# Seven-product down projection for the last row slice too, and two of the seventh slice's column slices put behind the last up projection

## The chip, the cores and the metric

The kernel runs on one core of a Trainium2 chip. The metric is the device time of one execution in microseconds; lower is better. Times of whole runs are medians of several executions; the profile is of one execution of its own.

## The reference, cut to what matters

A trunk of two pre-norm residual layers over x of 256 tokens by 2048 features in float32: the first mixes tokens with a convolution module, the second with a state-space layer, and each is followed by an MLP with 8192 hidden features. A last RMS norm ends it. Only the MLP of the second layer and the last norm are touched:

```
def mlp(h, w_up, w_down):
    a = jax.nn.relu(h @ w_up)          # 256 x 8192
    return (a * a) @ w_down            # 256 x 2048

x = x + mlp(rms_norm(x, mlp_norm[1]), w_up[1], w_down[1])
return rms_norm(x, final_norm)
```

## The kernel before, in words

**Products.** All weights stream from HBM in float32. Each tile is split into a high part (`hi`, a rounded copy made by ScalarE, L143) and a low part (`lo`, the difference, made by VectorE, L150). Every product is then three matmuls: high by high, high by low, low by high. The steps of the program are a list; one step is one tile of 1 MiB (128 partitions by 2048 numbers), fetched and split in two halves.

**Buffers that set the pace.** `run_steps` (L184) walks the half steps, asks for loads up to three steps ahead (L195) and for splits up to two steps ahead (L197). A plain tile lands in one of six `raw` half buffers by a DMA that SyncE issues; these DMAs are issued in program order (`fetch`, L98). There are four `hi` and four `lo` half buffers, so a split begins when TensorE has finished the half step four places before.

**The MLP** (`mlp`, L712). The 8192 hidden features are cut into eight row slices of 1024 (s = 0 to 7). `up(s)` is eight steps (four groups q of 256 hidden features, each in two parts kc): 16 matmuls with 512 columns and 16 with 256 in each step. After each second step the activation is made, squared and split, in one of two ways: `relu2` (L902) makes the squares for plain products, `relu2_forms` (L918) makes the four token-by-feature blocks of the squares and four sums and differences of them, eight "forms" in all. `down(s)` covers the four column slices n of 512 output columns with two steps each, 24 matmuls of 512 columns to a step; the sum is added to x by VectorE (`add_x`).

**Seven products** (`seven`, L725). For the column slices 0 and 1 of a row slice, the 2 by 2 block product is computed with seven block products in place of eight. The list it returns is called m[0] to m[7] here. Seven of these are steps with 12 matmuls of 512 columns; m[3] only loads. Their weight operands are running sums: chain X goes through m[0], m[2], m[4], m[7] and chain Y through m[3], m[6]. The first load of a chain is a plain one by SyncE into a `sum` tile; each later one is a DMA issued by GpSimd that adds the new weights onto the tile in SBUF (L120), and so waits until the tile was split. m[1] and m[5] are plain tiles. Three PSUM banks (p, q, r) collect the products, and seven VectorE instructions add or subtract them to four blocks of x ("takes", L743).

**Which slices use it.** `formed(s)` (L859) is true in the second layer for s = 0 to 6. The loop at L861 puts, for each s from 1 to 7, the eight steps u of `up(s)` between the steps of slice s-1: seven products for n = 0, 1 and `d`, the plain `down` of n = 2 and n = 3. After the loop `down(7)` (L871) is eight plain steps: n = 0, 1, 2 by `mm_t` and n = 3 by `consume_by_block` (L816), which finishes token block 0 ahead of block 1, so that the last norm can begin.

**The last norm.** `final_slice(n)` (L1635) is called when column slice n of x is complete, up to n = 2: two Squares with a sum on ScalarE, and one VectorE product of 128 by 1024 with the norm's gain `gF`. The call with n = 0 also allocates `gF` in the `blk` pool (six buffers, which also hold the activations `hT` in two and the squares `rT`, one or two to a slice) and loads it by a GpSimd DMA. `final_block(b)` scales and stores a token block.

**What sets the order.** The framework keeps data dependences and orders the instructions of each engine ahead of time, by priority and its own estimate of when each is ready; `high_priority` lifts splits and takes, and `behind` pins one instruction after another of the same engine.

Of the kernel before, what the change touches and what calls it, by code (L numbers as in the profile page):

```python
# [10 lines left out]
F32 = mybir.dt.float32  # L11
# [3 lines left out]
ALU = mybir.AluOpType  # L15
# [4 lines left out]
P = 128  # L20
# [4 lines left out]
NB = T // P  # L25
# [12 lines left out]
class Trunk:  # L38
    def __init__(self, ctx, tc, a, out):
        self.tc, self.nc, self.a = tc, tc.nc, a  # L40
        self.out = out[0].rearrange("(b p) c -> p b c", p=P)
        self.DF = a["mlp_w_up"].shape[2]
        pool = lambda name, bufs, **k: ctx.enter_context(tc.tile_pool(name=name, bufs=bufs, **k))
        self.const = pool("const", 1)
        self.w = pool("w", 3)
        self.blk = pool("blk", 6)
        self.tmp = pool("tmp", 4)
        self.small = pool("small", 2)
        self.acc = pool("acc", 2, space=PSUM)
        self.ms = pool("ms", 4, space=PSUM)  # L50
        self.dram = pool("dram", 1, space=DRAM)
        self.ctx = ctx
        self.t4_guard = tc.tile_pool(name="quad", bufs=4)
        self.quad = self.t4_guard.__enter__()
        self.wide = None
        self.steps = []
        self.pending = []
        self.bg = []
        self.rate = self.credit = 0
        self.raws, self.parts = {}, {}  # L60
        self.loaded = 0
        self.fetched = None
        self.barrier = self.lo_gate = None
        self.paced = False
        self.before_load = {}
# [19 lines left out]
    def add(self, view, shape, consume, pre=None):  # L85
        self.steps.append((view, shape, consume, pre))

    def add_chain(self, view, chain, consume=None):

        self.steps.append((view, chain, consume, "x"))  # L90

    def add_f(self, w2d, k0, c0, consume, pre=None):
        self.add(w2d[k0 * P:(k0 + 8) * P, c0:c0 + 256].rearrange("(k p) n -> p k n", p=P), [P, 8, 256], consume, pre)
# [9 lines left out]
    def load(self, i, half=None):  # L103
        view, shape, _, pre = self.steps[i]
        for kind in self.before_load.pop(i, ()):
            self.table(*kind)
        self.loaded = i + 1
        chain = None
        if pre == "x":
            chain, shape = shape, [P, 4, 512]  # L110
            if self.wide is None:
                self.t4_guard.__exit__(None, None, None)
                self.wide = self.ctx.enter_context(self.tc.tile_pool(name="wide", bufs=4))
        nk = shape[1] // 2
        for hf in (0, 1) if half is None else (half,):
            k = slice(hf * nk, hf * nk + nk)
            size = [P, nk] + list(shape[2:])
            if chain is not None:
                if hf in chain:
                    self.nc.gpsimd.dma_start(out=chain[hf], in_=view[:, k], accum_op=ALU.add)  # L120
                    continue
                raw = chain[hf] = self.wide.tile(size, F32, tag="wd", name="sum")
            else:
                raw = self.raws[2 * i + hf] = self.w.tile(size, F32, tag="raw", name="raw", bufs=6)
            if len(shape) == 4:
                for j in range(shape[2]):
                    self.fetch(raw[:, :, j, :], view[:, k, j, :])
            else:
                self.fetch(raw, view[:, k])

    def split(self, h, urgent=True):
        i, half = divmod(h, 2)
        _, chain, consume, pre = self.steps[i]
        if consume is None:
            return None
        if pre == "x":
            sl = chain[half]
        else:
            sl = self.raws.pop(h)
        hi = self.w.tile(list(sl.shape), F32R, tag="hi", name="hi", bufs=4)  # L140
        lo = self.w.tile(list(sl.shape), F32R, tag="lo", name="lo", bufs=4)
        with self.tc.high_priority(offset=URGENT if urgent else 0):
            self.nc.scalar.activation(hi, sl, AF.Copy)  # L143
            eng = self.nc.gpsimd if i in self.pool_lo else self.nc.vector
            if self.barrier is not None and h == 2 * self.barrier + 2:
                self.low_late = lambda: eng.tensor_tensor(out=lo, in0=sl, in1=hi.bitcast(F32), op=ALU.subtract)
                self.parts[h] = (hi, lo)
                return None
            with self.behind(self.lo_gate) if self.lo_gate is not None else nullcontext():
                ins = eng.tensor_tensor(out=lo, in0=sl, in1=hi.bitcast(F32), op=ALU.subtract)  # L150
# [102 lines left out]
    def mm_b(self, acc, act, hi, lo, b, c, first, last):  # L253

        mm = self.nc.tensor.matmul
        t = slice(b * P, (b + 1) * P)
        for kk in range(2):
            ak = act(kk)
            mm(acc, lhsT=ak[:, 0, t], rhs=hi[:, kk, c], start=first and kk == 0, stop=False)
            mm(acc, lhsT=ak[:, 0, t], rhs=lo[:, kk, c], start=False, stop=False)  # L260
            self.mm_last = mm(acc, lhsT=ak[:, 1, t], rhs=hi[:, kk, c], start=False, stop=last and kk == 1)

    def hsplit(self, raw, hi, lo):
        ins = self.nc.scalar.activation(hi, raw, AF.Copy)
# [447 lines left out]
    def mlp(self, layer, last_slice, last_block, hooks=None):  # L712
        w_up, w_dn = self.a["mlp_w_up"][layer], self.a["mlp_w_down"][layer]
        nsl = self.DF // 1024
        rT = {}

        def products(acc, s, i, hi, lo, half, first):
            mm = partial(self.nc.tensor.matmul, acc, skip_group_check=True)
            for jj in range(2):
# [2 lines left out]
                mm(lhsT=F[:, 0, i, :], rhs=lo[:, jj, :], start=False, stop=False)  # L722
                self.mm_last = mm(lhsT=F[:, 1, i, :], rhs=hi[:, jj, :], start=False, stop=half == jj == 1)  # L723

        def seven(s, n):  # L725


# [2 lines left out]
            x = self.x  # L730
# [4 lines left out]
            def part(form, bank, first, *takes):  # L735
                def consume(hi, lo, half):
                    if first and half == 0:
                        acc[bank] = self.bank([P, 512], name="m" + bank)
                    products(acc[bank], s, form, hi, lo, half, first)
                    if half == 1:  # L740
                        with self.tc.high_priority(offset=URGENT):
                            for c, op in takes:
                                self.tt(c, c, acc[bank], op)  # L743
                return consume
            A11, A22, A12, S1, S2, S3, S4 = range(1, 8)
            add, sub = ALU.add, ALU.subtract
# [7 lines left out]
                    lambda: load(B(1, 1), X, part(S2, "p", False, (c12, sub))),  # L754
                    lambda: plain(B(1, 1), part(S4, "r", False, (c12, sub))),
                    lambda: load(B(1, 1), Y, part(S3, "p", False, (c22, sub))),
                    lambda: load(B(1, 0), X, part(A22, "p", False, (c21, add)))]

        def up(s, only=None):
            for q in range(4):  # L760
# [25 lines left out]
                                act()  # L786
                    self.add_f(w_up, kc * 8, s * 1024 + q * 256, consume)

        def down(s, only=None):
            for n in range(NS):  # L790
                if only not in (None, n):
                    continue
                by_block = s == nsl - 1 and n == NS - 1
                for kc in range(2):
                    def consume(hi, lo, half, n=n, kc=kc):
                        if kc == 0 and half == 0:
                            rT["acc"] = self.acc2()
# [2 lines left out]
                        if not formed(s):  # L800
                            self.mm_t(acc, lambda kk: rT[s][:, k0 + kk], hi, lo,
                                      kc == 0 and half == 0, kc == 1 and half == 1)
                        else:
                            for kk in range(2):
                                for b in range(NB):
                                    F = rT[s][kc][:, half, :, 2 * kk + 1 - b, :]
                                    for i, (f, w) in enumerate(((0, hi), (0, lo), (1, hi))):
                                        self.mm_last = self.nc.tensor.matmul(  # L808
                                            acc[:, b, :], lhsT=F[:, f, :], rhs=w[:, kk, :],
                                            start=kc == half == kk == i == 0, stop=kc == half == kk == 1 and i == 2)  # L810
# [5 lines left out]
                    def consume_by_block(hi, lo, half, kc=kc):  # L816
# [7 lines left out]

                        def part(h, i):
                            with self.behind(self.mm_last):
                                self.mm_b(acc[i], lambda kk: rT[s][:, 2 * h + kk], *rT["w"][h], i > 0, cols[i], h == 0, h == 3)

                        part(h, 0)
                        if h < 2:  # L830
# [12 lines left out]
                    def consume_by_half(hi, lo, half, kc=kc):  # L843
# [2 lines left out]
                        h = kc * 2 + half  # L846
                        for i, (b, c) in enumerate(((0, slice(0, 512)), (1, slice(0, 256)), (1, slice(256, 512)))):
                            with self.behind(self.mm_last):
                                self.mm_b(rT["acc"][i], lambda kk: rT[s][:, 2 * h + kk], hi, lo, b, c, h == 0, h == 3)
                            if h == 3:  # L850
                                self.last_add(b, int(i == 2), c, rT["acc"][i])
                                if i:
# [3 lines left out]
                               consume if not by_block else consume_by_block if layer else consume_by_half,  # L856
                               (hooks or {}).get((nsl - 1 - s, n, kc)))

        formed = lambda s: layer == 1 and s < nsl - 1  # L859
        up(0)  # L860
        for s in range(1, nsl):  # L861
            if not formed(s - 1):
# [2 lines left out]
                continue  # L865
            m = seven(s - 1, 0)
            u = [partial(up, s, k) for k in range(8)]
            d = [partial(down, s - 1, n) for n in (2, 3)]
            for e in (u[0], m[0], u[1], m[1], u[2], m[2], u[3], d[0], u[4], m[3], m[4], u[5], m[5], u[6], d[1], m[6], u[7], m[7]):
                e()  # L870
        down(nsl - 1)  # L871

    def last_add(self, b, i, c, acc):

# [759 lines left out]

    def final_slice(self, n):  # L1635
        nc = self.nc
        if n == 0:
            self.block_ssq()
            self.gF = self.blk_tile([P, D], name="gF")
            nc.gpsimd.dma_start(out=self.gF, in_=self.a["final_norm"].unsqueeze(0).broadcast_to([P, D]))  # L1640
# [86 lines left out]
```

## Time and profile before

| | |
|---|---|
| runs of before | 1966.52, 1966.79 and 1967.05 us; median 1966.79 us |
| the profiled execution | 1968.06 us, of which the span from the first to the last instruction is 1966.3 us |
| granted TensorE clock | 0.999 |
| matmuls, VectorE, ScalarE and GpSimd instructions | 11520, 2093, 1249, 308 |
| moved by DMA | 457.95 MB, a mean of 233 GB/s |

The span holds the conv layer and its MLP, then the state-space layer, and, from about 1274 us, the MLP of the second layer. The loop of the row slices repeats every 85.4 us from about 1310 us on. The last turn of it (s = 7) runs from 1829.2 us to 1914.7 us, counted on TensorE; the eight plain steps of `down(7)` follow up to 1958.8 us, and what comes after is the last norm and the stores. In the views, PE is TensorE's matmuls and PEld its weight loads, DVE is VectorE, ACT ScalarE, POOL GpSimd, SP SyncE; a matmul's listed duration contains its pipeline and overlaps the next, so the pace is read from the starts.

### The profile page before, as it was taken

What the parts mean: (1) busy time and instruction counts of PE and PEld (TensorE: products, weight loads), DVE (VectorE), ACT (ScalarE), POOL (GpSimd) and SP (SyncE); (2) the same over time, 40 slices, a digit from 0 to 9 for tenths busy, and PEclk for the clock granted to TensorE, in tenths of its full rate; (3) what the DMA queues carried; (4) which work ended last, traced back from release to release, by engine and by line L of the source; (5) the groups of instructions that cost most, each with busy time, mean ns of one, the idle gap of its engine ahead of it and who ended that gap; (6) DMA issues with size and microseconds to landing.
All of it is one profiled execution on the core that took longest, in us unless ns stands there. A gap on an engine that the chain in (4) does not pass through costs nothing.

```text
span 1966.3 us, 30180 instructions
## 1 busy us (share of the span) xinstructions
PE 1947.6 (99%) x11520; PEld 1670.6 (85%) x11520; DVE 1490.9 (76%) x2093; ACT 1010.4 (51%) x1249; POOL 343.1 (17%) x308
## 2 busy tenths in 40 slices
PE   8999999999999999999999999999999999999998
PEld 8999788888888888888888788888888888888887
DVE  6899898888887677777557747577768777777765
ACT  6444655544444545454445445555555555555554
POOL 4899300000000222321101000001001010100100
PEclk9999999999999999999999999999999999999999
DMA  9668468777686868877898966679798897978883
GB/s 248 185 175 223 126 199 258 213 228 234 205 269 189 215 211 258 266 256 228 294 321 296 344 206 189 191 206 278 205 257 258 234 261 226 282 205 261 257 232 128
DMA packets 338096, 457.95 MB, mean 233 GB/s; under 512 B 16481, under 2 KB 218273, under 8 KB 334593
## 3 DMA queue, kind: packets, MB, share of 16 engines
q1 hardware_dynamic: 306800, 384.62, 60.9%
q0 software_dynamic: 27584, 66.85, 15.3%
q10 hardware_dynamic: 3568, 4.56, 0.8%
q8 instruction: 90, 1.47, 0.3%
q14 instruction: 54, 0.44, 0.1%
HBM read 429.44 MB, written 34.91 MB: 236 GB/s over the span
## 4 chain that ended last, share of the span: by engine, by line
PE 97%; DVE 1%; DMA 1%; issue 1%; POOL 0%; ACT 0%; SPq 0%; POOLq 0%; DVEq 0%; ACTq 0%
PE acc L226 24%; PE acc L229 12%; PE acc L249 10%; PE acc L250 10%; PE acc L251 10%; PE acc L808 8%; PE acc L238 3%; PE acc L240 3%; PE acc L239 3%; PE mp L721 1%; PE mp L722 1%; PE mp L723 1%; PE pk L511 1%; PE mr L721 1%; PE mr L722 1%; PE mr L723 1%
## 5 line engine op out<-in xcount | busy, mean ns | idle before, releaser
L143 ACT ACTIVATE hi<-raw 128x1024 fp32r<-128x1024 f32 x644 | 682.4, 1060 | 817.1 <-PE acc L251 331.1
L150 DVE TENSOR_TENSOR lo<-raw,hi 128x1024 fp32r<-128x1024 f32 x583 | 711.1, 1222 | 366.2 <-ACT hi L143 363.9
L226 PE MATMUL acc<-hT,hi 128*128 128x512 f32 x2048 | 513.5, 392 | 0.0
L226 PEld LDWEIGHTS acc<-hT,hi 128*128 128x128 f32 x2048 | 371.9, 189 | 70.7 <-issue 1.6
L229 PEld LDWEIGHTS acc<-hT,lo 128*128 128x128 f32 x2048 | 279.6, 190 | 20.0
L229 PE MATMUL acc<-hT,lo 128*128 128x256 f32 x2048 | 286.4, 282 | 0.0
L249 PE MATMUL acc<-hi,rT 128*128 128x512 f32 x544 | 212.9, 392 | 0.0
L250 PE MATMUL acc<-lo,rT 128*128 128x512 f32 x544 | 212.1, 390 | 0.0
L251 PE MATMUL acc<-hi,rT 128*128 128x512 f32 x544 | 211.7, 389 | 0.0
L120 POOL DMA_DIRECT2D sum<-in_mlp_w_down_dram x56 | 67.6, 1207 | 530.1 <-DVE lo L150 427.2
L150 POOL TENSOR_TENSOR lo<-raw,hi 128x1024 fp32r<-128x1024 f32 x60 | 144.0, 2415 | 30.3 <-ACT hi L143 28.0
L238 PE MATMUL acc<-hT,hi 128*128 128x256 f32 x512 | 146.2, 286 | 0.9 <-ACT hi L143 0.9
L239 PE MATMUL acc<-hT,hi 128*128 128x256 f32 x512 | 145.5, 286 | 0.0
L240 PE MATMUL acc<-hT,lo 128*128 128x256 f32 x512 | 145.1, 285 | 0.2 <-POOL lo L150 0.2
L948 DVE SCALAR_TENSOR_TENSOR cv<-vT,dw,cv 128x256 f32<-128x256 f32 x348 | 140.9, 482 | 2.6 <-ACT cv L554 2.2
L808 PE MATMUL acc<-hi,rT 128*128 128x512 f32 x448 | 140.4, 389 | 0.0
L249 PEld LDWEIGHTS acc<-hi,rT 128*128 128x128 f32 x544 | 102.1, 188 | 22.4 <-issue 1.6
L251 PEld LDWEIGHTS acc<-hi,rT 128*128 128x128 f32 x544 | 102.1, 188 | 21.5
L250 PEld LDWEIGHTS acc<-lo,rT 128*128 128x128 f32 x544 | 102.2, 188 | 20.9 <-issue 0.2
L150 DVE TENSOR_TENSOR lo<-sum,hi 128x1024 fp32r<-128x1024 f32 x70 | 85.5, 1221 | 27.9 <-ACT hi L143 27.2
L143 ACT ACTIVATE hi<-sum 128x1024 fp32r<-128x1024 f32 x70 | 74.3, 1062 | 56.2 <-PE acc L808 36.1
L238 PEld LDWEIGHTS acc<-hT,hi 128*128 128x128 f32 x512 | 98.8, 193 | 3.4 <-issue 2.1
(321 smaller groups left out, 2737.1 us busy)
## 6 DMA issues: line engine op xcount, KB each, us to landing
raw<-in_mlp_w_up_dram SPq DMA_DIRECT2D x256, 512.0 KB, 4.6
raw<-in_mlp_w_down_dram SPq DMA_DIRECT2D x228, 512.0 KB, 5.3
raw<-in_conv_w_in_dram SPq DMA_DIRECT2D x128, 256.0 KB, 3.6
raw<-in_ssm_w_glu_dram SPq DMA_DIRECT2D x64, 512.0 KB, 4.1
sum<-in_mlp_w_down_dram POOLq DMA_DIRECT2D x56, 512.0 KB, 8.5
raw<-in_conv_w_out_dram SPq DMA_DIRECT2D x32, 512.0 KB, 4.3
sum<-in_mlp_w_down_dram SPq DMA_DIRECT2D x28, 512.0 KB, 6.9
Vd<-bv POOLq DMA_DIRECT2D x16, 512.0 KB, 5.3
```

Of the source, the lines that this page charges most:

```text
L143: self.nc.scalar.activation(hi, sl, AF.Copy)
L150: ins = eng.tensor_tensor(out=lo, in0=sl, in1=hi.bitcast(F32), op=ALU.subtract)
L226: mm(accs[m], lhsT=hi[:, kk, cs[m]], rhs=xT(k0 + kk), start=first and kk == 0, stop=False)
L229: mm(accs[m][:, 0:T], lhsT=lo[:, kk, cs[m]], rhs=xT(k0 + kk)[:, 0, :], start=False, stop=last and kk == 3)
L238: mm(accs[m], lhsT=hi[:, kk, c], rhs=x[:, 0, :], start=first and kk == 0, stop=False)
L239: mm(accs[m], lhsT=hi[:, kk, c], rhs=x[:, 1, :], start=False, stop=False)
L240: mm(accs[m], lhsT=lo[:, kk, c], rhs=x[:, 0, :], start=False, stop=last and kk == 3)
L249: mm(acc[:, b, :], lhsT=ak[:, 0, t], rhs=hi[:, kk, :], start=first and kk == 0, stop=False)
L250: mm(acc[:, b, :], lhsT=ak[:, 0, t], rhs=lo[:, kk, :], start=False, stop=False)
L251: self.mm_last = mm(acc[:, b, :], lhsT=ak[:, 1, t], rhs=hi[:, kk, :], start=False, stop=last and kk == 1)
L808: self.mm_last = self.nc.tensor.matmul(acc[:, b, :], lhsT=F[:, f, :], rhs=w[:, kk, :], start=kc == half == kk == i == 0, stop=kc == half = ...
L948: return self.nc.vector.scalar_tensor_tensor(out=out, in0=a, scalar=s, in1=b, op0=op0, op1=op1)
```

## The change

1. `formed(s)` is true for all eight row slices of the second layer. So `up(7)` calls `relu2_forms`, its squares take two `blk` buffers, and the products of slice 7 with n = 0, 1 go through `seven`. `final_slice(0)` and `final_slice(1)` are called after the last of the seven products, m[7], has been taken into x.
2. In the loop's last turn (s = 7) the plain `down` of slice 6 for n = 2, 3 is left out, and a new list behind the loop holds it, one step at a time (`part`) between the seven products of slice 7. The order behind the loop is: m[0], d0a, m[1], d0b, m[2], d1a, m[3], m[5], d1b, m[4], d2a, m[6], d2b, m[7], and then n = 3 of slice 7 by block as before. Here d0 and d1 are n = 2 and 3 of slice 6, d2 is n = 2 of slice 7, and a and b are their two steps. `final_slice(2)` is the first to be called, after d2b.
3. `mm_b` takes its activation by (kk, b), and `squares` picks the block from the formed or the plain layout. The loop at L804 to L810 becomes two calls of `mm_b`, one for each token block.
4. `gF` is loaded at the first call of `final_slice`, whatever its n.
5. `add_chain`, `load` and `split` learn a second kind of chain, "v", in which a plain load is added on VectorE. No call uses it: `seven` still passes no `by`, so its chains are "x" as before.

```
-            mm(acc, lhsT=ak[:, 0, t], rhs=hi[:, kk, c], start=first and kk == 0, stop=False)
+            ak = act(kk, b)
+            mm(acc, lhsT=ak[:, 0, :], rhs=hi[:, kk, c], start=first and kk == 0, stop=False)
...
+        def squares(s, k0):
+            if formed(s):
+                return lambda kk, b: rT[s][k0 // 4][:, k0 // 2 % 2, :, 2 * kk + 1 - b, :]
+            return lambda kk, b: rT[s][:, k0 + kk, :, b * P:(b + 1) * P]
...
+                        if last(s) and takes[-1][0] is None:
+                            for n in takes[-1][1]:
+                                last_slice(n)
...
-                    lambda: load(B(1, 0), X, part(A22, "p", False, (c21, add)))]
+                    lambda: load(B(1, 0), X, part(A22, "p", False, (c21, add), (None, (n, n + 1))))]
...
-        def down(s, only=None):
+        def down(s, only=None, part=None):
...
-                for kc in range(2):
+                for kc in range(2) if part is None else (part,):
...
-        formed = lambda s: layer == 1 and s < nsl - 1
+        formed = lambda s: layer == 1
+        last = lambda s: s == nsl - 1
...
-            d = [partial(down, s - 1, n) for n in (2, 3)]
+            d = [partial(down, s - 1, n) for n in (2, 3)] if not last(s) else [lambda: None] * 2
...
-        down(nsl - 1)
+        if not formed(nsl - 1):
+            return down(nsl - 1)
+        m = seven(nsl - 1, 0)
+        d = [partial(down, s, n, kc) for s, n in ((nsl - 2, 2), (nsl - 2, 3), (nsl - 1, 2)) for kc in range(2)]
+        for e in (m[0], d[0], m[1], d[1], m[2], d[2], m[3], m[5], d[3], m[4], d[4], m[6], d[5], m[7], partial(down, nsl - 1, 3)):
+            e()
...
     def final_slice(self, n):
-        if n == 0:
+        if self.gF is None:
```

More of the change, by code (lines that the diff above doesn't have):

```diff
@@ L54, in __init__ @@
         self.quad = self.t4_guard.__enter__()
-        self.wide = None
+        self.wide = self.gF = None
         self.steps = []
@@ L86, in add, with add_chain @@
         self.steps.append((view, shape, consume, pre))
-    def add_chain(self, view, chain, consume=None):
-        self.steps.append((view, chain, consume, "x"))
+    def add_chain(self, view, chain, consume=None, by="x"):
+        self.steps.append((view, chain, consume, by))
     def add_f(self, w2d, k0, c0, consume, pre=None):
@@ L108, in load @@
         chain = None
-        if pre == "x":
+        if pre in ("x", "v"):
             chain, shape = shape, [P, 4, 512]
@@ L118, in load @@
             if chain is not None:
-                if hf in chain:
+                if hf in chain and pre == "x":
                     self.nc.gpsimd.dma_start(out=chain[hf], in_=view[:, k], accum_op=ALU.add)
                     continue
-                raw = chain[hf] = self.wide.tile(size, F32, tag="wd", name="sum")
+                if hf in chain:
+                    raw = self.raws[2 * i + hf] = self.w.tile(size, F32, tag="raw", name="raw", bufs=6)
+                else:
+                    raw = chain[hf] = self.wide.tile(size, F32, tag="wd", name="sum")
             else:
@@ L135, in split @@
             return None
-        if pre == "x":
+        if pre in ("x", "v"):
             sl = chain[half]
+            if h in self.raws:
+                self.tt(sl, sl, self.raws.pop(h), ALU.add)
         else:
@@ L255, in mm_b @@
         mm = self.nc.tensor.matmul
-        t = slice(b * P, (b + 1) * P)
         for kk in range(2):
-            ak = act(kk)
-            mm(acc, lhsT=ak[:, 0, t], rhs=hi[:, kk, c], start=first and kk == 0, stop=False)
-            mm(acc, lhsT=ak[:, 0, t], rhs=lo[:, kk, c], start=False, stop=False)
-            self.mm_last = mm(acc, lhsT=ak[:, 1, t], rhs=hi[:, kk, c], start=False, stop=last and kk == 1)
+            ak = act(kk, b)
+            mm(acc, lhsT=ak[:, 0, :], rhs=hi[:, kk, c], start=first and kk == 0, stop=False)
+            mm(acc, lhsT=ak[:, 0, :], rhs=lo[:, kk, c], start=False, stop=False)
+            self.mm_last = mm(acc, lhsT=ak[:, 1, :], rhs=hi[:, kk, c], start=False, stop=last and kk == 1)
     def hsplit(self, raw, hi, lo):
@@ L742, in consume @@
                             for c, op in takes:
-                                self.tt(c, c, acc[bank], op)
+                                if c is not None:
+                                    self.tt(c, c, acc[bank], op)
+                        if last(s) and takes[-1][0] is None:
+                            for n in takes[-1][1]:
+                                last_slice(n)
                 return consume
@@ L803, in consume @@
                         else:
[L804 to L810, printed above, removed]
+                            for b in range(NB):
+                                self.mm_b(acc[:, b, :], squares(s, k0), hi, lo, b, slice(0, 512),
+                                          kc == 0 and half == 0, kc == 1 and half == 1)
                         if kc == 1 and half == 1:
@@ L826, in part @@
                             with self.behind(self.mm_last):
-                                self.mm_b(acc[i], lambda kk: rT[s][:, 2 * h + kk], *rT["w"][h], i > 0, cols[i], h == 0, h == 3)
+                                self.mm_b(acc[i], squares(s, 2 * h), *rT["w"][h], i > 0, cols[i], h == 0, h == 3)
                         part(h, 0)
@@ L848, in consume_by_half @@
                             with self.behind(self.mm_last):
-                                self.mm_b(rT["acc"][i], lambda kk: rT[s][:, 2 * h + kk], hi, lo, b, c, h == 0, h == 3)
+                                self.mm_b(rT["acc"][i], squares(s, 2 * h), hi, lo, b, c, h == 0, h == 3)
                             if h == 3:
```

## The prediction

> **What bounds the kernel now.** I read the page's busy line and its chain of work first, then the windows of the stages that the change touches.
>
> ```profile
> span 1966.3 us, 30180 instructions
> PE 1947.6 (99%) x11520; PEld 1670.6 (85%) x11520; DVE 1490.9 (76%) x2093; ACT 1010.4 (51%) x1249; POOL 343.1 (17%) x308
> PE 97%; DVE 1%; DMA 1%; issue 1%; POOL 0%; ACT 0%; SPq 0%; POOLq 0%; DVEq 0%; ACTq 0%
> ...
> 1741.20:1774.20 33.00, 33.00 (x176) 28.45 (x175) 27.70 (x36) 20.59 (x25) 4.82 (x4) 1.00 0.90 237
> 1823.40:1908.90 85.50, 85.50 (x438) 73.12 (x438) 60.91 (x68) 46.96 (x52) 10.21 (x9) 1.00 0.87 247
> 1914.90:1958.00 43.10, 43.10 (x211) 36.50 (x211) 28.30 (x33) 20.73 (x32) 0.94 (x1) 1.00 0.32 109
> ```
>
> In the windows the columns are the length, then the busy time of PE, PEld, DVE, ACT and POOL, the granted clock, the share of the DMA engines and GB/s. PE is busy for 99% of the span and is 97% of the chain. In the loop's last turn (1823 to 1909 us) and in the plain steps behind it, its busy time is the whole window at clock 1.00. So the stage is bound by matmuls alone, and a matmul less is worth its slot, as long as nothing else becomes late. The price of a slot is in the chain in order of time:
>
> ```profile
> 1859.88 10.91 PE acc L808 x48
> 1870.79 1.81 PE acc L226 x8
> 1872.60 0.95 PE acc L229 x8
> 1873.55 1.84 PE acc L226 x8
> 1875.39 0.95 PE acc L229 x8
> 1876.35 0.23 PE mp L721
> ...
> 1879.09 1.81 PE acc L226 x8
> ```
>
> 48 matmuls of 512 columns take 10.91 us: 0.2273 us each. An up step is 1.81 + 0.95 + 1.84 + 0.95 = 5.55 us, a seven-product step of 12 matmuls lasts from 1876.35 to 1879.09, 2.73 us, a plain down step 5.45 us.
>
> The Trainium skill (Perfetto Trace Analysis, Identifying the Most-Contended Engine) says that matmul busy time is a poor measure of TensorE's distance to its roofline, and that the share of weight loads should be read in its place; here that is 85%. By this rule TensorE would have some 15% of holes. The trace does not bear it out for the pace: with 0.2273 us from start to start and no idle time before a group, streaming the columns is what lasts, not the loads.
>
> **The change part by part.**
>
> *Matmuls.* The plain n = 0, 1 of slice 7 were 2 slices x 4 half steps x 12 = 96 matmuls of 512 columns; the seven products are 7 x 12 = 84. The change removes 12 x 0.2273 = **2.73 us**. All else on TensorE is the same work in another order: the four steps of slice 6 that leave the loop's last turn come back behind it. So this is all that can be won on TensorE; the norm at the end keeps its steps.
>
> *The squares of slice 7.* They are now needed early. m[0] is only one step (m[7] of slice 6) behind the last up step, and its second half uses the forms of the last two groups. Behind the last up step of slice 6 the same activation ran like this:
>
> ```profile
> 1825.70 0.95 PE acc L229 x8
> ...
> 1826.70 0.59 ACT L924 ACTIVATE t<-acc 128x512 f32<-128x512 f32 x1
> 1831.05 0.63 ACT L264 ACTIVATE rT<-u 128x512 fp32r<-128x512 f32 x1
> 1832.57 0.68 DVE L265 TENSOR_TENSOR rT<-u,rT 128x512 fp32r<-128x512 f32 x1
> ```
>
> TensorE was done at 1826.65. The high part stood at 1831.68, 5.03 us later, and the low part at 1833.25, 6.60 us later, because urgent splits and takes go first. In the new order TensorE needs them after m[7] (2.73 us), half of m[0] (1.36 us) and three more matmuls (0.68 us): the high part at 4.77 us, the low part two slots later at 5.23 us. The high part is 0.26 us late; the low part, after that shift, is due at 5.49 and comes at 6.60, 1.11 us late. In printed order this costs 1.37 us. But the order on TensorE is not always that of the program:
>
> ```profile
> 1282.74 2.46 PE L226 MATMUL acc<-hT,hi 128*128 128x512 f32 x10
> 1285.04 0.40 PE L229 MATMUL acc<-hT,lo 128*128 128x256 f32 x2
> 1285.27 1.09 PE L226 MATMUL acc<-hT,hi 128*128 128x512 f32 x4
> ```
>
> The program asks for eights; here the groups of two steps were mixed. If d0a, whose squares of slice 6 are long ready, is mixed into m[0] the same way, nothing is lost. Ends: 0 and 1.37; I take the middle, **+0.7 us**, since each end has a row.
>
> *More work on DVE and ACT.* `relu2_forms` in place of `relu2`, seven takes, and the splits of 15 steps in 63.5 us (8 x 5.55 + 7 x 2.73) without the long d steps between. The first row of the windows with DVE at 27.70 of 33.00 us is such a stretch of u0 to u3 and m[0] to m[2], without a d: 84%, and PE had no gap. The dense stretch now lasts longer, but is no denser, so I cost it at nothing; it would cost what DVE lacks if it had over 33.00 us of work in such a stretch.
>
> *The chains' accumulating DMAs.* Each waits until the sum before it was split, and has to land before its own split.
>
> ```profile
> L143 ACT ACTIVATE hi<-sum 128x1024 fp32r<-128x1024 f32 x14 | 14.9, 1062 | 13.1 <-PE acc L808 9.8 <-PE mp L723 2.2 <-PE mq L723 1.0
> L150 DVE TENSOR_TENSOR lo<-sum,hi 128x1024 fp32r<-128x1024 f32 x14 | 17.1, 1222 | 7.7 <-ACT hi L143 7.5
> ...
> DMA to landing us min/median/max: 9.1/10.8/11.1
> ```
>
> A split is 1.06 + 1.22 = 2.3 us; the accumulates of 1860 to 1893 us landed after 9.1 to 11.1 us. The shortest distances in the new order are m[2] to m[4] in the last turn, which loses d0 from between, and m[0] to m[2] behind it. A split starts four half steps ahead. For the first, m[1]'s second half, u2, m[2], u3 and u4 lie between the split and the use of m[4]: 1.36 + 5.55 + 2.73 + 5.55 + 5.55 = 20.7 us, less two splits, 16.1 us. For the second: 2.77 + 2.73 + 2.73 + 5.45 + 2.73 + 5.45 = 21.9, less two splits, 17.3 us. Both exceed 11.1, so nothing, unless the DMA engines as a whole fall behind (a rival below). GpSimd issues these in order, with `gF` among them: that waits for the last up projection to free `hT`, and what is queued behind it are accumulates of the tail. SyncE's loads also stand in order, so the plain load of the new m[0], which waits for m[6]'s split, holds up those of d0a and m[1]; they are due over 10 us later.
>
> *The end.* `final_slice(0)` and `(1)` move behind m[7], beside the last down steps. That is one take, four Squares and two products with `gF` that must be done before block 0 is added:
>
> ```profile
> L939 DVE TENSOR_TENSOR x<-x,mp 128x512 f32<-128x512 f32 x7 | 4.8, 679 | 0.0
> L939 DVE TENSOR_TENSOR x<-x,gF 128x1024 f32<-128x1024 f32 x3 | 3.7, 1225 | 0.8 <-ACT junk L298 0.8
> ...
> 1951.53 0.17 DVE L945 TENSOR_SCALAR ssa<-ssa 128x2 f32<-128x2 f32 x1
> 1954.49 0.69 DVE L939 TENSOR_TENSOR x<-x,acc 128x512 f32<-128x512 f32 x1 [2.80 <-PE acc L261]
> 1955.27 0.63 ACT L880 ACTIVATE junk<-x 128x512 f32<-128x512 f32 x1 [5.11 <-DVE x L939]
> ```
>
> On DVE that is 0.68 + 2 x 1.23 = 3.1 us into an idle 2.80 us, so 0.3 us at most by this row; and slice 2's own product and add lie one step earlier now, which makes room. On ACT four Squares of 0.6 to 0.8 us go into 5.11 us idle. Ends 0 and 1 (should they sit between the adds of the last block); I take **+0.3 us**.
>
> *Sum.* -2.73 + 0.7 + 0.3 = **-1.7 us**. Against the profiled execution, 1968.06 us with its span of 1966.3 us and 1.8 us around it, that gives 1966.3 us. That execution is 1.3 us above the median of the runs shown, 1966.79 us; the forecast goes by the median: **1965.1 us**, -0.09%. A measurement of this kernel can tell about 0.2%, 3.9 us, from no change, and even the bare 2.73 us is less.
>
> **The rivals.**
>
> *A: the new waits eat the gain.* If m[0] waits the full 1.37 us, the low part comes later still because m[0] releases its splits earlier than an up step did (one or two more urgent ones of 1.2 us ahead of it), and the end costs 1 us, the sum is -2.73 + 1.37 + 1.2 + 1.0 = +0.8: 1967.6 us. For it: the order of the rows above, urgent first. Against it: TensorE may fill with d0a. Its stretch is 1965.9 to 1968.0. The rule on weight loads, taken at its word, would end here too: with another limit in the holes, twelve matmuls less gain nothing, 1966.8 us.
>
> *B: slower, because loads fall behind.* From u4 to m[7] (4 x 5.55 + 4 x 2.73 = 33.1 us) nine tiles are wanted, from m[0] to m[5] behind it (27.3 us) eight, and `gF`: 18 x 1.0486 = 18.9 MB in 60.4 us, 312 GB/s, where a whole turn of the loop ran at 247. What DMA can do:
>
> ```profile
> 1859.90:1870.80 10.90, 10.90 (x49) 9.01 (x49) 6.92 (x8) 4.95 (x7) 2.47 (x3) 1.00 1.08 363
> 1870.80:1893.00 22.20, 22.20 (x121) 19.27 (x121) 15.61 (x17) 13.09 (x14) 2.31 (x2) 1.00 1.09 294
> ...
> ACT hi L143 <- DMA raw<-in_mlp_w_up_dram: 3.3, 1, 3.3
> ...
> DMA to landing us min/median/max: 3.6/7.3/17.4
> ```
>
> For B: with 1.08 and 1.09 the engines were full there, some loads took 17.4 us (1820 to 1909 us), and ACT once waited 3.3 us for one. Against it: they delivered (10.9 x 363 + 22.2 x 294) / 33.1 = 317 GB/s, more than is wanted, and PE had no gap even so. Loads run ahead by 17.4 - 7.3 = 10 us of lateness that cost PE nothing. So B decides below 18.9 MB / 70.4 us = 268 GB/s. At the loop's 247 the tiles take 76.5 us, 6.1 us over: -1.7 + 6.1 = +4.4, 1971.2 us. More accumulating tiles than in that stretch (four of 17, and gF) make this possible.
>
> The Trainium skill (DMA: Bandwidth & Descriptors, Where 436 GB/s comes from) puts the limit for traffic from HBM at about 358 GB/s for a core. By it the 18.9 MB take an estimated 53 us of the 60.4, and B does not occur; the 363 GB/s of the row above agrees with it, the 294 shows that mixed traffic can stay below.
>
> *C: the forms do not do what they say.* An unused "v" chain comes with the diff; had it been used, DVE would add 8 x 1.2 us and GpSimd none. As no call passes it, the chains stay, and I give this nothing.
>
> **How the numbers follow.** Forecast (1963.9 to 1965.9; all of the 2.73 us kept down to 0.9): 0.57. A: 0.25. B: 0.15, of which 0.12 over 1970.7 and the rest just below. A gain beyond 2.73 us, for which I find no place but a shorter end: 0.03. The range leaves out that and the upper part of B: 1963.8 to 1970.5 us. Faster by over 0.2% (below 1962.9): 0.02. Slower by over 0.2% (above 1970.7): 0.12. Between: 0.86.
>
> **What would show it.** The matmul count falls by 12 to 11508. Between the last up matmul and the first plain step behind the loop, a PE wait on DVE's or ACT's rT of up to 1.4 us, or d0a's matmuls between those of m[0], decides the second term. The DVE idle before the add of block 0 (2.80 us) shrinks to near nothing, while the steps behind the last matmul keep their length. ACT's waits for DMA in the stretch from u4 to m[5], and PE gaps that follow them, speak for B; landings over 17 us are its sign. I am wrong if PE shows gaps of over 2 us elsewhere, or if the last matmul ends over 3 us earlier relative to the loop's start.

## The result: slower, and outside the range

| | before | after |
|---|---|---|
| median of 6 runs each | 1966.86 us | 1974.74 us |
| lowest to highest | 1966.46 to 1967.92 us | 1973.78 to 1975.91 us |
| ratio, 95% interval | | 1.0040 [1.0027, 1.0053] |
| profiled execution | 1968.06 us | 1973.78 us |
| its span | 1966.3 us | 1971.9 us |

The change costs 7.9 us of median; 1965.1 us was forecast. The spans of the two profiled executions differ by 5.6 us, and it is these that are taken apart here (that of before was 1.2 us above its median, that of after 1.0 us below). First the page of after: busy time and chain.

```profile
PE 1947.4 (99%) x11508; PEld 1668.7 (85%) x11508; DVE 1503.6 (76%) x2120; ACT 1016.8 (52%) x1259; POOL 352.6 (18%) x316
PE 92%; DMA 4%; DVE 2%; issue 1%; POOL 1%; ACT 0%; SPq 0%; POOLq 0%; DVEq 0%; ACTq 0%
```

The matmul count fell by 12, as the change says. But the chain of work that ended last, 97% PE and 1% DMA before, is now 92% PE and 4% DMA. The windows of after show where (columns as in the prediction):

```profile
1820.97:1865.00 44.03, 44.03 (x239) 38.15 (x238) 31.91 (x40) 22.99 (x26) 7.29 (x6) 1.00 0.94 244
1865.00:1877.57 12.57, 10.83 (x49) 8.56 (x48) 9.66 (x14) 8.92 (x11) 2.41 (x2) 0.86 0.99 237
1877.57:1926.00 48.43, 48.43 (x231) 40.67 (x230) 39.39 (x48) 27.32 (x31) 7.91 (x7) 1.00 0.91 273
1926.00:1937.00 11.00, 7.63 (x32) 5.58 (x31) 4.99 (x5) 5.32 (x6) 2.40 (x2) 1.00 1.06 278
```

PE is busy for the whole of two windows (and of what follows, up to 1964 us) and has holes in the two others, 1865 to 1877.6 and 1926 to 1937 us; in the first of these the granted clock drops too. The waits of PE from 1300 us on name what ended the holes (total, times, longest); the same view of before has no row at all:

```profile
PE mp L726 <- ACT hi L149: 3.6, 2, 2.6
PE mp L727 <- DVE lo L156: 1.5, 2, 0.8
```

The timeline of PE in after (start, duration, instruction, idle time before it) gives the two places:

```profile
1866.50 0.39 PE L728 MATMUL mp<-hi,rT 128*128 128x512 f32 x1
1867.87 0.49 PE L726 MATMUL mp<-hi,rT 128*128 128x512 f32 x1 [0.97 <-ACT hi L149]
1869.12 0.50 PE L727 MATMUL mp<-lo,rT 128*128 128x512 f32 x1 [0.76 <-DVE lo L156]
...
1870.41 3.57 PE L232 MATMUL acc<-hT,hi 128*128 128x512 f32 x8
1873.82 1.12 PE L235 MATMUL acc<-hT,lo 128*128 128x256 f32 x8
...
1926.85 0.39 PE L264 MATMUL acc<-hi,rT 128*128 128x512 f32 x1
1929.85 0.50 PE L726 MATMUL mp<-hi,rT 128*128 128x512 f32 x1 [2.61 <-ACT hi L149]
...
1933.85 0.50 PE L726 MATMUL mp<-hi,rT 128*128 128x512 f32 x1
1935.11 0.50 PE L727 MATMUL mp<-lo,rT 128*128 128x512 f32 x1 [0.76 <-DVE lo L156]
```

The first place is m[4] of slice 6, in the loop's last turn, where its second half begins; the second is m[4] of slice 7 behind the loop, both halves. Read by starts, with 0.23 us as the normal step: the first costs 1.14 + 1.02 + 0.11 of waiting and 3.41 - 1.81 = 1.60 at a halved clock, 3.9 us together. The second costs 2.77 + 0.11 + 1.03 + 0.11 us and some hundredths on the matmuls that follow, 4.1 us. With the 12 matmuls (-2.73) and the end (+0.26, shown below) this makes 3.9 + 4.1 - 2.73 + 0.26 = +5.5 of the 5.6 us. Nothing else is left to explain in this execution.

What the splits waited for stands in the chain in order of time of after (start, length, what):

```profile
1851.23 15.42 DMA sum<-in_mlp_w_down_dram
1866.76 1.06 ACT hi L149
1867.84 1.24 DVE lo L156
...
1914.11 18.52 DMA sum<-in_mlp_w_down_dram
1932.73 1.07 ACT hi L149
1933.83 1.24 DVE lo L156
```

Both times it is an accumulating DMA of chain X, landed 15.4 and 18.5 us after it was issued. These two are second halves of m[4]. The longest wait of the second place, 2.61 us, is for the first half; ScalarE's timeline has its split:

```profile
1928.74 1.06 ACT L149 ACTIVATE hi<-sum 128x1024 fp32r<-128x1024 f32 x1 [6.07 <-DMA sum<-in_mlp_w_down_dram]
```

That DMA was issued at 1913.4 us and landed after 15.3 us. Why these were issued so late and landed so late is in GpSimd's own timeline of after (idle time before an instruction and what ended it in brackets):

```profile
1848.41 1.20 POOL L121 DMA_DIRECT2D sum<-in_mlp_w_down_dram  x1 [14.62 <-DMA sum<-in_mlp_w_down_dram]
1849.78 3.68 POOL L121 DMA_DIRECT2D sum<-in_mlp_w_down_dram  x3 [0.16 <-issue]
...
1911.64 4.92 POOL L121 DMA_DIRECT2D sum<-in_mlp_w_down_dram  x4 [14.35 <-DMA sum<-in_mlp_w_down_dram]
```

Four accumulates go out in one bunch, and what released the first of them is a DMA, not a split: it is m[6]'s, which waits for the plain load of chain Y (m[3]). m[4]'s two stand behind m[6]'s. In before the last turn ran the other way round; GpSimd's timeline there:

```profile
1847.55 1.20 POOL L120 DMA_DIRECT2D sum<-in_mlp_w_down_dram  x1 [13.80 <-DMA raw<-in_mlp_w_down_dram]
...
1849.28 1.29 POOL L120 DMA_DIRECT2D sum<-in_mlp_w_down_dram  x1
1865.17 1.20 POOL L120 DMA_DIRECT2D sum<-in_mlp_w_down_dram  x1 [14.60 <-DMA sum<-in_mlp_w_down_dram]
```

Here m[4]'s two are out by 1849.3 us and m[6]'s follow 16 us later. The order of GpSimd's instructions is laid down ahead of time. By their times and by what released them the pairs of accumulates stand like this:

| | order of the pairs in GpSimd's queue |
|---|---|
| before, every turn | m[2], m[4], m[6], m[7] |
| after, turns s = 1 to 6 | m[2], m[4], m[6], m[7] |
| after, last turn | m[2], **m[6]**, m[4], m[7] |
| after, behind the loop | m[2], **m[6]**, m[4], m[7] |

m[6] is used two up steps later than m[4] in the turn, so its pair has no hurry. In after the first split of m[2] ended at 1847.2 us, 3.3 us before m[4]'s first DMA went out (1850.5), as VectorE's timeline shows:

```profile
1846.00 1.22 DVE L156 TENSOR_TENSOR lo<-sum,hi 128x1024 fp32r<-128x1024 f32 x1
...
1847.74 1.22 DVE L156 TENSOR_TENSOR lo<-sum,hi 128x1024 fp32r<-128x1024 f32 x1
```

The landing times of the bunches in after, by the view of the tile `sum` (min, median, max; the last three of the first bunch, then the four of the second):

```profile
DMA to landing us min/median/max: 8.6/11.9/15.4
...
DMA to landing us min/median/max: 9.0/13.6/18.5
```

The first of the first bunch landed after 6.3 us. So within a bunch the time to landing grows by 2.3 to 3.5 us from place to place, and the third and fourth places were m[4]'s.

### The profile page after: what moved, and what is told of

Same layout as the page of the kernel before. It is cut to its first block, busy times and chain, and to the rows that moved or that the text cites. A ratio compares the mean times of both kernels' runs of the same rounds, so it can differ in the third digit from the quotient of the medians.

```text
span 1971.9 us, 30216 instructions
## 1 busy us (share of the span) xinstructions
PE 1947.4 (99%) x11508; PEld 1668.7 (85%) x11508; DVE 1503.6 (76%) x2120; ACT 1016.8 (52%) x1259; POOL 352.6 (18%) x316
## 4 chain that ended last, share of the span: by engine, by line
PE 92%; DMA 4%; DVE 2%; issue 1%; POOL 1%; ACT 0%; SPq 0%; POOLq 0%; DVEq 0%; ACTq 0%
PE acc L232 23%; PE acc L235 12%; PE acc L255 10%; PE acc L256 10%; PE acc L257 9%; PE acc L244 3%; PE acc L246 3%; PE acc L245 3%; PE acc L264 3%; PE acc L265 3%; PE acc L266 3%; DMA sum<-in_mlp_w_down_dram 2%; PE mp L727 1%; PE mp L726 1%; PE mp L728 1%; PE pk L516 1%
## 5 line engine op out<-in xcount | busy, mean ns | idle before, releaser
L232 PEld LDWEIGHTS acc<-hT,hi 128*128 128x128 f32 x2048 | 372.9, 189 | 71.0 <-issue 1.6
L255 PE MATMUL acc<-hi,rT 128*128 128x512 f32 x496 | 194.2, 392 | 0.0
L256 PE MATMUL acc<-lo,rT 128*128 128x512 f32 x496 | 193.4, 390 | 0.0
L257 PE MATMUL acc<-hi,rT 128*128 128x512 f32 x496 | 193.0, 389 | 0.0
L121 POOL DMA_DIRECT2D sum<-in_mlp_w_down_dram x64 | 77.3, 1263 | 566.3 <-DVE lo L156 447.8
L156 DVE TENSOR_TENSOR lo<-sum,hi 128x1024 fp32r<-128x1024 f32 x80 | 97.5, 1221 | 41.8 <-ACT hi L149 41.2
L149 ACT ACTIVATE hi<-sum 128x1024 fp32r<-128x1024 f32 x80 | 84.7, 1061 | 72.5 <-PE acc L266 28.5
L255 PEld LDWEIGHTS acc<-hi,rT 128*128 128x128 f32 x496 | 93.1, 188 | 20.7 <-issue 1.6
L257 PEld LDWEIGHTS acc<-hi,rT 128*128 128x128 f32 x496 | 93.1, 188 | 19.4
L256 PEld LDWEIGHTS acc<-lo,rT 128*128 128x128 f32 x496 | 93.2, 188 | 19.1 <-issue 0.2
L265 PE MATMUL acc<-lo,rT 128*128 128x512 f32 (+1 forms) x288 | 108.9, 378 | 0.0
L264 PE MATMUL acc<-hi,rT 128*128 128x512 f32 (+1 forms) x288 | 108.8, 378 | 0.0
```

The costliest lines, as they stand in the source:

```text
L232: mm(accs[m], lhsT=hi[:, kk, cs[m]], rhs=xT(k0 + kk), start=first and kk == 0, stop=False)
L255: mm(acc[:, b, :], lhsT=ak[:, 0, t], rhs=hi[:, kk, :], start=first and kk == 0, stop=False)
L256: mm(acc[:, b, :], lhsT=ak[:, 0, t], rhs=lo[:, kk, :], start=False, stop=False)
L257: self.mm_last = mm(acc[:, b, :], lhsT=ak[:, 1, t], rhs=hi[:, kk, :], start=False, stop=last and kk == 1)
L264: mm(acc, lhsT=ak[:, 0, :], rhs=hi[:, kk, c], start=first and kk == 0, stop=False)
L265: mm(acc, lhsT=ak[:, 0, :], rhs=lo[:, kk, c], start=False, stop=False)
```

## The experiments

Three theories stood against each other:
- **Q**: the order in GpSimd's queue. m[6]'s pair, ahead of m[4]'s, holds m[4]'s up and takes the first landings.
- **D**: the distance. With d0 gone from between m[2] and m[4], m[4]'s accumulate has too little time in any order.
- **B**: rival B of the prediction, the DMA engines as a whole deliver too little.

Behind the first runs of after, the kernels ran in two groups on two chips, each beside runs of before on its chip, so they are compared by their ratio to before. The first group has the three pinned kernels and m[4] added on VectorE (before: 33 runs, median 1967.83 us), the second the other four (before: 13 runs, 1967.57 us).

| kernel | median, runs | ratio to before, 95% | span | PE waits, 1300 to 1950 us |
|---|---|---|---|---|
| after, first time | 1974.74 (6) | 1.0040 [1.0027, 1.0053] | 1971.9 | 5.1 |
| after, again | 1974.55 (6) | 1.0035 [1.0023, 1.0047] | 1973.2 | 5.8 |
| order pinned in turn and tail | 1964.87 (11) | 0.9986 [0.9977, 0.9995] | 1963.0 | none |
| pinned in the turn only | 1969.16 (10) | 1.0007 [0.9998, 1.0017] | 1967.9 | 2.8 |
| pinned behind the loop only | 1968.87 (10) | 1.0006 [0.9997, 1.0015] | 1966.9 | 1.8 |
| m[4] added on VectorE | 1966.34 (10) | 0.9992 [0.9983, 1.0001] | 1962.9 | none |
| the move alone | 1975.76 (5) | 1.0042 [1.0029, 1.0054] | 1974.0 | 4.2 |
| seven products alone | 1980.42 (4) | 1.0069 [1.0055, 1.0083] | 1978.2 | 9.2 |
| before, with m[6]'s pair first | 1971.82 (8) | 1.0024 [1.0014, 1.0034] | 1969.6 | 3.5 |

### The order pinned, in both places

```
+                    with self.behind(self.summed) if i in self.pin and self.summed is not None else nullcontext():
+                        self.summed = self.nc.gpsimd.dma_start(out=chain[hf], in_=view[:, k], accum_op=ALU.add)
...
+        self.pin = range(self.turn, len(self.steps))
```

Each accumulate from the last turn on is put behind the one before it in the program, which gives m[2], m[4], m[6], m[7] in both places. Nothing else changes.

> GpSimd's accumulating DMAs are pinned to the program's order in the loop's last turn and behind it, so that m[4]'s pair stands ahead of m[6]'s; nothing else differs from the changed kernel (1974.7 us). Theory Q (queue order: m[4]'s pair waits behind m[6]'s, which waits for the Y load, and then lands in a bunch of four): both TensorE stalls (3.9 us with the slow clock behind it in the turn, 3.4 us behind it) go, 1964 to 1968 us. Theory D (distance: without d0 between, m[4]'s pair lands too late in any order): the stall in the turn shrinks only by the 2 to 4 us that the pair is issued earlier and does not vanish, 1970 us or more. Theory B (the DMA engines as a whole are too slow there): what is moved ahead makes other loads as late, 1973 us or more.

It took 1964.87 us, 0.9986 [0.9977, 0.9995] of before: the only version whose interval lies below 1. PE waits for nothing from 1300 us on. GpSimd's timeline of this kernel:

```profile
1846.64 1.20 POOL L123 DMA_DIRECT2D sum<-in_mlp_w_down_dram  x1 [13.73 <-DVE lo L158]
1848.37 3.68 POOL L123 DMA_DIRECT2D sum<-in_mlp_w_down_dram  x3 [0.53 <-DVE v L962]
...
1906.90 4.92 POOL L123 DMA_DIRECT2D sum<-in_mlp_w_down_dram  x4 [14.41 <-DVE lo L158]
```

The first is now released by a split, so it is m[4]'s, and its second follows at the head of a bunch of three. The landings of these four, then of the four of 1906.9 us, by the view of the tile `sum`:

```profile
DMA to landing us min/median/max: 7.3/9.5/12.7
...
DMA to landing us min/median/max: 8.9/13.8/18.7
```

m[4]'s took the first places; the slow ones, up to 18.7 us, are now m[6]'s, for which nobody waits yet. Two windows of this kernel, around those bunches:

```profile
1850.00:1862.00 12.00, 12.00 (x69) 10.48 (x68) 9.05 (x12) 7.10 (x9) 4.46 (x4) 1.00 1.11 245
1907.00:1933.00 26.00, 26.00 (x117) 21.52 (x116) 19.92 (x19) 12.74 (x12) 7.22 (x6) 1.00 1.09 276
```

The DMA engines are as full as in after (shares 1.11 and 1.09, 245 and 276 GB/s; 1.06 and 278 in after's second hole), and PE has no gap. Theory B falls, and D with it: d0 is still away. Q holds. The kernel's span is 3.3 us below that of before; 0.85 us of this it already led at m[2]'s accumulate (1829.97 against 1830.82 us in before), the rest is -2.73 + 0.27.

### Pinned in one place only

The same edit, with `self.pin = range(self.turn, self.after_up)`, then with `range(self.after_up, len(self.steps))`, where `after_up` is the first step behind the loop.

> The same pinning in the loop's last turn alone. Theory Q: the first stall goes with its slow clock, the second stays: 1974.7 - 3.9 = 1970.8 us. Theory D: about 1973 us or more. Theory B: the second stall grows by what the first loses, 1974 us.

> The same pinning behind the loop alone. Theory Q: the first stall stays, the second goes: 1974.7 - 3.4 = 1971.3 us. Theory B: no change, 1974.7 us.

Each keeps one of the two stalls. The waits of PE, first with the turn pinned, then with the tail pinned:

```profile
PE mp L728 <- ACT hi L151: 2.0, 1, 2.0
PE mp L729 <- DVE lo L158: 0.8, 1, 0.8
```

```profile
PE mp L729 <- DVE lo L158: 1.2, 2, 0.8
PE mp L728 <- ACT hi L151: 0.6, 1, 0.6
```

The ratios are 1.0007 and 1.0006: each of the two stalls, alone, is worth some 4 us against the version without any (1.0007 - 0.9986 = 0.0021 of 1967 us). The medians lie below what was expected (1970.8 and 1971.3 us). Added to the version without any, both would give 1.0027, at the lower end of the interval of after, 1.0040 [1.0027, 1.0053]. In neither of these executions did the granted clock fall at the stall, while both profiles of after show one spell at half clock; with its 1.6 us (0.0008) the sum is 1.0035.

### m[4]'s addend by VectorE

```
-                    lambda: load(B(1, 1), X, part(S2, "p", False, (c12, sub))),
+                    lambda: load(B(1, 1), X, part(S2, "p", False, (c12, sub)), "v" if s >= nsl - 2 else "x"),
```

The unused "v" chain of the diff for the m[4] of slices 6 and 7: a plain load by SyncE, and an add on VectorE.

> m[4] of slices 6 and 7 as a v chain: SyncE loads it plainly and VectorE adds it (two more instructions of 1.2 us for each), no accumulating DMA; the others stay. Theories Q and D: m[4] waits for no accumulate, the load may run ahead of the sum's split, both stalls go: 1964 to 1968 us. Theory B: as many bytes are loaded, so the stalls stay for the most part: 1971 us or more.

No PE wait is left, and the span is the shortest, 1962.9 us. But its runs go from 1964.75 to 1967.27 us, and the ratio, 0.9992 [0.9983, 1.0001], is not told from 1. The stall goes when m[4] no longer stands behind m[6] on GpSimd. This fits Q; it fits D as well, since m[4] waits for no accumulate at all here. Why its runs spread more than those of the pinned version is open.

### The move alone, and the seven products alone

The move alone: `formed = lambda s: layer == 1 and s < nsl - 1` again, and behind the loop

```
+        if layer == 1:
+            down(nsl - 2, 2)
+            down(nsl - 2, 3)
+        return down(nsl - 1)
```

> Slice 7 keeps its plain products, and slice 6's n = 2, 3 still go behind the last up projection: the move without the seven products. No matmul is saved, and no chain runs behind the loop. Theory Q: the first stall alone, since GpSimd's order in the turn is again m[6]'s pair first; 1966.9 + 2 to 4 us, 1969 to 1971 us. Theory that the seven products are what costs: no loss, 1966.9 us.

It came out at 1.0042 [1.0029, 1.0054], as slow as the whole change, though it has no chain behind the loop: more than any theory gave it. The waits of PE and a window of it:

```profile
PE mp L726 <- ACT hi L149: 3.6, 1, 3.6
PE mp L727 <- DVE lo L156: 0.6, 1, 0.6
```

```profile
1872.00:1874.00 2.00, 1.85 (x4) 1.16 (x5) 2.00 (x2) 1.97 (x4) 0.74 (x1) 0.50 0.54 98
```

m[6]'s pair is ahead of m[4]'s here too, and `gF`'s megabyte goes out between m[4]'s two (at 1851.8 us); the second of m[4] took 18.2 us to land. Then the clock, the column before the DMA share, was granted at 0.50 for 6.8 us: 4 matmuls in the 2 us shown, where 9 would fit. By starts the waits cost 4.6 us, already above the 2 to 4 us of theory Q, and the matmuls at half clock 2.6 us more.

The seven products alone: d0 and d1 stay in the last turn, and the tail is the list without them.

```
-            d = [partial(down, s - 1, n) for n in (2, 3)] if not last(s) else [lambda: None] * 2
+            d = [partial(down, s - 1, n) for n in (2, 3)]
...
+        d = [partial(down, nsl - 1, 2, kc) for kc in range(2)]
+        for e in (m[0], m[1], d[0], m[2], d[1], m[3], m[5], m[4], m[6], m[7], partial(down, nsl - 1, 3)):
```

m[4] and m[7] lie so close in this list that m[7]'s addend is asked for before m[4]'s second half is split, so this half uses a sum with the next addend already on it. The instructions and bytes are those of the full computation, but that split waits for one accumulate more.

> The seven products of slice 7 with slice 6's n = 2, 3 left in the turn: m[0], m[1], d2a, m[2], d2b, m[3], m[5], m[4], m[6], m[7] behind the loop. Theory Q with distance: no stall in the turn (its order is m[4]'s pair first there), a longer one behind it, since only d2b and m[5], 8.2 us, lie between m[2] and m[4], and m[6]'s pair goes first: 5 to 12 us of stall, 1969 to 1976 us. Theory that the move is what costs: 1964 us.

It is the slowest, 1.0069 [1.0055, 1.0083]. In the turn, with d0 back, the order is the old one (m[4] at 1846.5, m[6] at 1860.2 us) and there is no stall. Behind the loop, m[6] is first again, and PE waits, by the costliest row of its waits:

```profile
PE mp L726 <- ACT hi L149: 7.8, 2, 7.7
```

One wait alone is 7.7 us, longer than any in after. It ends with the split of m[4]'s second half; GpSimd's and ScalarE's timelines:

```profile
1937.84 2.43 POOL L121 DMA_DIRECT2D sum<-in_mlp_w_down_dram  x2 [10.61 <-DMA sum<-in_mlp_w_down_dram]
```

```profile
1944.02 3.90 ACT L149 ACTIVATE hi<-sum 128x1024 fp32r<-128x1024 f32 x4 [5.01 <-DMA sum<-in_mlp_w_down_dram]
```

m[4]'s own accumulate had landed at 1937.5 us (issued at 1926.03, 11.5 us to landing). The split waited for m[7]'s, issued at 1937.84 and landed after 6.1 us. So some 6 of the 7.7 us belong to the extra addend, and the clock was granted at 0.50 for 13.7 us from 1942 us on. The time of this kernel, above the 1969 to 1976 us that Q with distance gave, is therefore no measure of Q or D in the tail. What it does show is the turn: with d0 back the order is the old one, and there is no stall.

### The order alone, in the kernel before

Before's own last turn, with m[6]'s pair issued ahead of m[4]'s:

```
+        if i == self.m4:
+            ahead, sums = self.steps[self.m6][:2]
+            for hf in range(2):
+                self.summed = self.nc.gpsimd.dma_start(out=sums[hf], in_=ahead[:, 2 * hf:2 * hf + 2], accum_op=ALU.add)
...
```

Further on in the edit, m[6]'s own place issues nothing, and m[4]'s pair is put behind m[6]'s.

> The kernel before with one change: in the loop's last turn m[6]'s accumulating pair is issued ahead of m[4]'s, as in the changed kernel; d0 stays between m[2] and m[4], so that m[4] is used 10.9 us later. Theory Q alone (the order costs by itself): 2 to 4 us over the kernel before, 1969 to 1971 us. Theory Q with distance (the order hurts only where d0 is gone): no TensorE gap, within 1 us of the kernel before.

1.0024 [1.0014, 1.0034], 4.3 us slower by the order alone, with d0 in its place and no seven products on slice 7. GpSimd's timeline:

```profile
1858.52 1.19 POOL L118 DMA_DIRECT2D sum<-in_mlp_w_down_dram  x1 [25.47 <-DMA sum<-in_mlp_w_down_dram]
1859.91 1.20 POOL L118 DMA_DIRECT2D sum<-in_mlp_w_down_dram  x1 [0.21 <-issue]
1860.64 2.93 POOL L127 DMA_DIRECT2D sum<-in_mlp_w_down_dram  x2
```

GpSimd stood 25.5 us at the head of its queue for a load, and m[4]'s two (L127) went out at 1860.6 in place of 1847.6 us. They landed after up to 17.1 us, and PE waited 2.0 us for ACT's and 1.5 us for DVE's part of those splits. Q does not need D. The hold-up is larger than in after, 13 us instead of some 3: m[3]'s plain load goes out at 1852.1 us here, behind d0's loads, and at 1841.5 us in after. d0's two steps between m[2] and m[4], 10.9 us of TensorE, take up most of it.

The second series of after, in this group, came out at 1.0035 [1.0023, 1.0047], where 1.004 was expected. Its profile has both stalls again, with no drop of the clock behind the first, but one behind the second: after a wait of 3.87 us the clock was granted at 0.50 from 1931.2 to 1934.6 us.

## Why the prediction was wrong, point by point

**Matmuls: right.** 11520 to 11508, and 2.73 us are there to be had: the pinned kernel, from m[2] of the last turn on, is 2.73 - 0.27 us shorter than before.

**The squares of slice 7: the lower end held.** +0.7 us was taken between 0 and 1.37; it cost 0. TensorE filled with d0a, as the mixed groups of the prediction suggested. After's PE timeline, behind the last up step:

```profile
1901.92 0.39 PE L726 MATMUL mq<-hi,rT 128*128 128x512 f32 x1
1902.14 0.39 PE L726 MATMUL mp<-hi,rT 128*128 128x512 f32 x1
...
1902.60 0.39 PE L265 MATMUL acc<-lo,rT 128*128 128x512 f32 x1
```

Matmuls of two seven-product steps (`mq`, `mp`) and of d0a (`acc`) follow one another without idle time.

**More work on DVE and ACT: right.** 1820.97 to 1865.00 us and 1877.57 to 1926.00 us are wholly busy on PE, with DVE at 31.91 of 44.03 and 39.39 of 48.43 us. No wait there.

**The end: the size came out by luck.** VectorE's timeline of after:

```profile
1959.83 0.69 DVE L956 TENSOR_TENSOR x<-x,acc 128x512 f32<-128x512 f32 x1 [0.55 <-PE acc L266]
...
1964.14 0.42 DVE L956 TENSOR_TENSOR x<-x,acc 128x256 f32<-128x256 f32 x1 [0.44 <-PE acc L266]
```

The idle 2.80 us before block 0 shrank to 0.55, so what moved there did fit: the term, some 3.1 us of work into 2.80 us idle, cost nothing. From the last add to the end of the span it is 1971.9 - 1964.14 = 7.76 us, in before 1966.3 - 1958.80 = 7.50, +0.26 where +0.3 was forecast; the pinned kernel shows +0.27. But this lies elsewhere: from this add to VectorE's last step it is 2.5 us in both, and the last group of SyncE's stores begins 5.24 us before the end in before and 5.50 us in after. The prediction said that these last steps would keep their length; why they did not is open.

**The chains' accumulating DMAs: this step failed.** The prediction said "Both exceed 11.1, so nothing". Its distance was about right: 16.1 us were worked out for m[2] to m[4] in the turn, and what TensorE allowed was 15.7 us (the second split of m[2] ended at 1848.96, and the landing was needed at 1864.66, the two parts of a split before the use of its low part at 1866.96). Wrong was what it set beside the distance. It took the landings of before, 9.1 to 11.1 us, and tacitly the issue at the moment of the split. In after the DMA went out 2.3 us after the split (1851.23 against 1848.96), because m[6]'s pair stood ahead of it, and landed after 15.4 us, because it was the fourth of a bunch: 17.7 us against 15.7.

Behind the loop the prediction worked out m[0] to m[2] as the shortest distance, 17.3 us. Late was m[4]'s pair there too: its first DMA went out at 1913.4 us, 2.3 us after the split of m[2] (1911.1), and landed after 15.3 us, 17.6 together, where TensorE allowed 14.9 (1926.0, one ScalarE part of a split ahead of the matmul due at 1927.08). That is less than any distance in the prediction, in part because TensorE's order puts the first matmul of m[4] ahead of 11 matmuls of d1b that stand before m[4] in the program; they ran right behind the wait, from 1930.19 us on.

The text did say that GpSimd issues in order and that distances lose d0, but it looked only at what it knew to be new in the queue, `gF` and the accumulates of the tail, and not at whether the old ones would keep their order.

**Rival B: the sign and over half of the size, not the mechanism.** 1971.2 us was forecast for it, +4.4 against the measured +7.9 us. The waits of ACT for a DMA and the gaps of PE behind them came as B would show them, landings over 17 us too. But the engines delivered as much in the pinned kernel, where PE had no gap. Nor are the 363 GB/s, which the prediction read as agreeing with a limit of about 358, a limit here: with m[4] added on VectorE, plain loads alone moved a mean of 387 GB/s from 1904 to 1908 us.

**The chances** were 0.12 for slower by over 0.2%. No rival changed the order of a queue. The change gives the framework a new program to order, and the views of before can't show that order; what they could show is how little room there was for a wrong one: m[4] had some 5 us to spare by the prediction's own terms (16.1 - 11.1), less than two places in a bunch at 2.3 to 3.5 us each.

What stays open: why the order comes out this way. It is the new one in the turn of each kernel that takes d0 and d1 out and leaves the order free (after, the move alone, the kernel pinned only behind the loop), and the old one where they stay (before, the seven products alone). That the framework expects Y's plain load earlier once d0 is gone, and so puts its pair first, fits this, but its estimates were not looked at.

## What to carry to other kernels

Moving a step in the program can turn round the order of instructions that it doesn't touch: after a move, list the order of each queue of transfers, and pin those that are due first to the front. In these runs the price of an accumulating DMA was its place in the queue and in its bunch, not the median landing; a distance has to hold against the last of a bunch. When a change loses what it should have won, look first for the instruction that waits at the head of an in-order queue, and who stands behind it.

## What the runs showed of the hardware that was not expected

**Accumulates in a bunch land one after another.** Four of 512 KB, issued 0.7 to 1.4 us apart, landed after 6.3, 8.6, 11.9 and 15.4 us, and in the tail after 9.0, 11.9, 15.3 and 18.5 us. As moments, issue and landing added, these are 1854.7, 1858.4, 1862.4 and 1866.6 us, and 1920.6, 1924.6, 1928.7 and 1932.6 us: one every 3.7 to 4.2 us, although they were issued closer together. The four of before that the prediction read as 9.1 to 11.1 us (issued at 1865.17, 1866.57, 1870.72 and 1873.48, landed after 9.1, 11.1, 10.4 and 11.1 us) also came down 3.4 to 3.5 us apart. So the spacing could be read before the change; the time to landing hid it, since there they were issued further apart.

**Waits can halve TensorE's clock, but not every time.** In after, two waits of 0.97 and 0.76 us within 2.6 us were followed by eight matmuls in 3.41 us, at a granted 0.50 in their middle. The second profile of after had waits of 0.54, 0.66 and 0.75 us at the same place and kept 1.00; the turn-pinned kernel kept it behind 2.01 us, and after itself behind 2.61 us. Waits of 3.58 us (the move alone), 3.87 us (after, second profile) and 7.65 us (the seven products alone) each came with 0.50, and in the move alone the clock fell within 2 us of the wait's beginning. These spells at 0.50 last 3.4 us in both profiles of after, 6.8 us in the move alone and 13.7 us in the seven products alone: one, one, two and four times 3.41 us. The Trainium skill (TensorE: Matmul & The Clock Gate, Part 1: The HAM clock gate) tells of two rates, full and half, set by windows of about 3.4 us that run free of the program, with the half rate after an idle window. The two rates, the length of the spells and a phase that differs from run to run agree with these rows; that a whole window has to be idle doesn't, since after's own first stall had matmuls between its waits. What decides was not settled.
